# Expert results stored by token and choice, and the next mixers' input products by token tile and by half

## The chip, the cores and the metric

The kernel runs on one core of a Trainium2 chip. The metric is device microseconds of one execution. TensorE (PE) multiplies matrices, VectorE (DVE) and ScalarE (ACT) do elementwise work, GpSimd (POOL) does small operations and issues the DMAs that take a list of row indices, SyncE (SP) issues nearly all other loads and stores.

## The reference, cut to what matters

512 tokens of 1024 channels go through two blocks in fp32. The first block has two layers, a mixer (fox attention, then MLA attention) followed by 16 experts, of which each token uses the two best of its best group. The second block puts 16 meta tokens in front and has a Hyena convolution mixer and a differential attention.

```python
h = rmsnorm(x, mix_norm[i]) * (1.0 + sc1) + sh1
y = fox_mixer(h, ...) if i % 2 == 0 else mla_mixer(h, ...)
x = x + g1 * y
h = rmsnorm(x, ffn_norm[i]) * (1.0 + sc2) + sh2
x = x + g2 * hier_moe(h, ...)        # y = sum over a token's two choices of weight * expert(h)
...
y = rmsnorm_2(h, norm_pre[i])        # second block: h is 16 meta tokens, then x
u = y @ w_in + b_in                  # hyena: four streams of 2048 channels
x0, x1, v = jnp.split(dwconv_centred(u[..., :3 * D_INNER], conv_w, conv_b), 3, axis=-1)
```

So behind each expert layer stand the same steps: y of both choices is summed, multiplied by g2, added to x, and x is normed for the next mixer's input product.

## The kernel before, in words

**Order of the phases.** Fox attention of layer 0 (to about 350 us), experts of layer 0 (355 to 641), MLA (641 to 880), experts of layer 1 (920 to 1222), Hyena (1207 to 1890), differential attention (to the end). The instructions of a phase are written in Python; a scheduler then orders them on each engine by readiness and priority, and each engine works through its own list strictly in order. SyncE's queue, and POOL's, are such lists too. Tiles have tags with a fixed number of buffers, so a load may start only when the reader of the buffer's earlier content is done.

**Products in fp32** are three matmuls on split numbers (`mm3`, lines 147 to 153): each operand is a high part (ACT cast, line 125) and a low part (DVE subtraction, line 128). Weights come as `raw` (load by SyncE, line 133), then `whi` and `wlo`. `rsqrt` (lines 114 to 119) is one DVE operation and POOL's power.

**Experts** (`moe`, line 1096). The routing gives each token and choice a slot in one of 16 blocks of 128 (one per expert); blocks 16 to 22 take an expert's 129th slot and beyond. `tix` (line 1185) holds the token of each slot, for an empty slot the index of a spare row. For each block `gather` (line 1204) fetches 128 rows of `hd` by an indirect DMA (line 1206), `expert_in` and `expert_out` (lines 1061, 1076) make the products, ACT copies the result to `yo` (line 1092), and POOL issues an indirect DMA that adds the rows of `yo` into `yd` (line 1093). Since rows are added, `yd`, of 512 + 128 rows, must be zero first: `moe_fill` (lines 939 to 947), called twice in fox attention (lines 625, 627), stores 2560 KB of zeros into `yd` and 512 KB into the spare rows of `hd`, for each layer. Behind the 16 experts an If (line 1247) takes the first overflow block, and a For_i (line 1250) over `n_ov` takes further ones. Between the experts, and after that loop, parts of Hyena's filter network run as filler (`fil`, lines 1393 to 1409).

**The seam to MLA** (`mla`, from line 704). `moe_sum` (line 1261) loads `yd` by tile of 128 tokens. `moe_norm` (line 338) is a generator over the four tiles: y times g2 (lines 346 and 359), x plus y (345), square (ACT, into h; tile 0 by DVE, line 354), rsqrt, x times r times gain (360), plus shift (362), then `put_T` (line 368) transposes and splits. The input product of 672 columns goes by column half: `gemm_tok` (line 777) takes all four token tiles for columns 0 to 335, then all four for the rest; `evac_in` (line 766) copies to `ct` (line 774).

**The seam to Hyena** (`hyena`, from line 1430). The same, with no shift. Then the constants (`cw`, `hb`, `cb`, line 1467) and four tables (line 1297, by POOL's queue) are loaded. `streams(ct)` (line 1506) makes the four streams of a channel tile: `proj` (line 1483) takes both token halves of 264 columns for one stream, with 24 matmuls each, `conv` (line 1493) is a three-tap convolution on the result, copied out by ACT (line 1499). `long_conv` (line 1522; its first matmul is at line 1545) follows.

## Time and profile before

| | us |
|---|---|
| median of 3 runs | 2627.5 (2625.51 to 2631.35) |
| the profiled execution | 2622.27 |
| its span in the trace | 2620.5 |
| PE busy | 2384.9 (91%) |
| DVE busy | 1887.5 (72%) |
| ACT busy | 1507.4 (58%) |
| POOL busy | 255.4 (10%) |

The page of the profile gives busy time by engine, the span in 40 slices, the DMA queues, the chain of work that ended last and the costliest groups of instructions. The trace behind it answers for any stretch: windows (busy time of each engine, granted clock of PE, share of the DMA engines), waits (which line waited for what, how long in all), the timeline (one line for each instruction or run of like ones) and groups of instructions by shape. "A <- B" in a wait means that A stood until B was done. An engine with q behind its name is its queue of DMA and control instructions.

### The profile page before, as it was taken

Reading aid. Unit: us, or ns where it says so; the run is one execution under the profiler, and the core shown is the slowest. Engines: PE = TensorE matmul, PEld = TensorE weight load, DVE = VectorE, ACT = ScalarE, POOL = GpSimd, SP = SyncE. Lnnn points to the kernel's source line nnn. Section 1 sums busy time; section 2 is a strip of 40 time slices with the busy share of each in tenths; the row PEclk is TensorE's granted clock in tenths of the full one; section 3 lists DMA queues with packets and bytes.
Section 4 is the critical chain, followed back from the end, with each engine's and each line's share of the span. In section 5 each row is a group of like instructions: output and inputs, shape, how many; then the busy total and the mean of one; then the engine's idle time right before and its main releaser. Section 6 shows DMA issues by size and latency. Waiting matters only on the chain.

```text
span 2620.5 us, 40079 instructions
## 1 busy us (share of the span) xinstructions
PE 2384.9 (91%) x14775; PEld 1978.0 (75%) x14775; DVE 1887.5 (72%) x4037; ACT 1507.4 (58%) x2958; POOL 255.4 (10%) x264
## 2 busy tenths in 40 slices
PE   6889988897899979995999999999799999999988
PEld 5667767775766767774999999997577777777666
DVE  7888877886788768885566666664657778777755
ACT  5575757885567368874444444443336666665652
POOL 1100112221122022211000000000100000000000
PEclk8899989999899989997999999999899999999989
DMA  7776668997211289985323222224322121111232
GB/s 262 249 254 203 219 187 267 322 316 228 88 37 49 75 256 315 327 282 196 103 90 92 92 93 92 91 73 131 116 89 69 41 73 69 65 49 69 88 108 82
DMA packets 130271, 387.00 MB, mean 148 GB/s; under 512 B 23226, under 2 KB 34730, under 8 KB 129304
## 3 DMA queue, kind: packets, MB, share of 16 engines
q1 hardware_dynamic: 115640, 330.31, 37.1%
q0 software_dynamic: 12128, 45.38, 7.2%
q10 hardware_dynamic: 2304, 8.72, 0.8%
q8 instruction: 117, 1.92, 0.3%
q14 instruction: 82, 0.67, 0.1%
HBM read 330.58 MB, written 53.77 MB: 147 GB/s over the span
## 4 chain that ended last, share of the span: by engine, by line
PE 45%; DVE 4%; ACT 2%; issue 2%; DMA 1%; POOL 0%; POOLq 0%; SPq 0%; ACTq 0%; DVEq 0%
PE ps_mm L150 11%; PE ps_mm L151 10%; PE ps_mm L152 10%; PE ps_sc L1822 1%; PE ps_b L152 1%; PE ps_b L150 1%; PE ps_b L151 1%; PE ps_sc L1823 1%; PE ps_tp L1852 1%; ACT whi L125 1%; PE ps_tl L1764 1%; PE ps_tp L1565 1%; DVE wlo L128 1%; PE ps_pv L150 1%; PE ps_tq L1852 1%
## 5 line engine op out<-in xcount | busy, mean ns | idle before, releaser
L128 DVE TENSOR_TENSOR wlo<-raw,whi 128x1024 fp32r<-128x1024 f32 (+3 forms) x426 | 501.3, 1185 | 244.0 <-ACT whi L125 230.6
L125 ACT CAST whi<-raw 128x1024 fp32r<-128x1024 f32 (+3 forms) x426 | 433.2, 1022 | 246.9 <-PE ps_mm L152 91.1
L150 PE MATMUL ps_mm<-hT,whi 128*128 128x264 f32 x1024 | 294.7, 288 | 0.8 <-ACT hT L125 0.8
L151 PE MATMUL ps_mm<-hT,whi 128*128 128x264 f32 x1024 | 293.4, 287 | 0.8 <-DVE hT L128 0.8
L152 PE MATMUL ps_mm<-hT,wlo 128*128 128x264 f32 x1024 | 292.0, 285 | 0.0
L150 PE MATMUL ps_mm<-whi,hT 128*128 128x512 f32 x512 | 206.9, 406 | 6.9 <-DVE zg L1757 5.9
L151 PE MATMUL ps_mm<-wlo,hT 128*128 128x512 f32 x512 | 205.9, 403 | 0.0
L152 PE MATMUL ps_mm<-whi,hT 128*128 128x512 f32 x512 | 205.6, 403 | 0.0
L151 PEld LDWEIGHTS ps_mm<-hT,whi 128*128 128x128 f32 x1024 | 194.7, 190 | 1.1 <-DVE hT L128 1.1
L150 PEld LDWEIGHTS ps_mm<-hT,whi 128*128 128x128 f32 x1024 | 194.1, 190 | 1.6 <-ACT hT L125 1.6
L152 PEld LDWEIGHTS ps_mm<-hT,wlo 128*128 128x128 f32 x1024 | 194.4, 190 | 0.0
L151 PE MATMUL ps_mm<-wlo,un 128*128 128x384 f32 (+1 forms) x376 | 140.4, 375 | 10.0 <-DVE wlo L128 9.8
L150 PE MATMUL ps_mm<-whi,un 128*128 128x384 f32 (+1 forms) x376 | 141.4, 379 | 4.4 <-ACT whi L125 1.7
L152 PE MATMUL ps_mm<-whi,un 128*128 128x384 f32 (+1 forms) x376 | 138.3, 372 | 0.0
L1830 ACT ACTIVATE P<-P,nm 128x528 f32<-128x528 f32 x128 | 94.4, 737 | 70.7 <-DVE P L1827 69.1
L1499 ACT ACTIVATE u<-ps_mm,hb 128x264 f32<-128x264 f32 x96 | 46.2, 481 | 137.4 <-PE ps_mm L152 137.4
L119 POOL TENSOR_TENSOR r<-rs,mhalf 128x4 f32<-128x4 f32 (+1 forms) x72 | 79.1, 1102 | 400.1 <-DVE rs L118 381.5
L150 PEld LDWEIGHTS ps_mm<-whi,hT 128*128 128x128 f32 x512 | 97.0, 190 | 27.2 <-DVE zg L1757 6.8
L150 PE MATMUL ps_mm<-whi,xgT 128*128 128x512 f32 x264 | 107.1, 406 | 8.2 <-ACT xgT L125 8.2
L219 DVE CUSTOM_DVE_ANT_0 ada<-ada,crow 128x1024 f32<-128x1024 f32 x80 | 97.5, 1219 | 22.1 <-DMA ada<-in_w_ada_dram 21.4
L152 PEld LDWEIGHTS ps_mm<-whi,hT 128*128 128x128 f32 x512 | 97.0, 190 | 18.1
L151 PEld LDWEIGHTS ps_mm<-wlo,hT 128*128 128x128 f32 x512 | 96.8, 189 | 17.5 <-issue 0.2
(594 smaller groups left out, 6379.4 us busy)
## 6 DMA issues: line engine op xcount, KB each, us to landing
raw<-in_moe_gu_dram SPq DMA_DIRECT2D x136, 512.0 KB, 7.7
ada<-in_w_ada_dram SPq DMA_DIRECT2D x96, 512.0 KB, 4.3
raw<-in_moe_dn_dram SPq DMA_DIRECT2D x68, 512.0 KB, 7.0
raw<-in_hy_w_dram SPq DMA_DIRECT2D x64, 512.0 KB, 3.5
raw<-in_da_w_dram SPq DMA_DIRECT2D x64, 512.0 KB, 4.6
raw<-in_fox_w_dram SPq DMA_DIRECT2D x32, 384.0 KB, 4.6
hs<-ht ACTq DMA_DIRECT2D x16, 532.0 KB, 7.3
H<-hs SPq DMA_DIRECT2D x16, 532.0 KB, 3.4
```

Of the source, the lines that this page charges most:

```text
L119: self.lastpow = nc.gpsimd.tensor_tensor(out, t, self.mhalf[:in_.shape[0]].to_broadcast(list(in_.shape)), op=ALU.pow)
L125: nc.scalar.copy(hi, src)
L128: return nc.vector.tensor_sub(lo, src, hi.bitcast(F32))
L150: r = nc.tensor.matmul(o, a[0], b[0], start=first, stop=False)
L151: nc.tensor.matmul(o, a[0], b[1], start=False, stop=False)
L152: self.lastmm = nc.tensor.matmul(o, a[1], b[0], start=False, stop=last)
L219: nc.vector.tensor_tensor_reduce(out=t, in0=t, in1=self.crow, op0=ALU.mult, op1=ALU.add, scale=1.0, scalar=0.0, accum_out=v[:, j:j + 1])
L1499: A.activation(u[:, 1 + hs.start:1 + hs.stop], p, AF.Identity, bias=hb[:, c:c + 1])
L1565: nc.tensor.transpose(p[:, cs], ab[:, f, cs], self.ident)
L1764: nc.tensor.matmul(tp[32 * j:32 * j + 16, 0:64], xt[:, k, :], w[:, c0 + j * 64:c0 + (j + 1) * 64], start=(k == 0), stop=(k == KD - 1))
L1830: nc.scalar.activation(P, P, AF.Exp, bias=nm_, scale=-1.0, accum_out=sum_)
L1852: nc.tensor.transpose(p[0:n, qt * 128:(qt + 1) * 128], Ps[qt][:, kt * 128:kt * 128 + n], self.ident)
```

## The change

1. `yd` has 2 x 512 rows: a block's result row is stored, not added, at row choice x 512 + token. Empty slots get an index past the end, which the bounds check of the DMA skips. A third column of the table (`tix`) keeps the token for the gathers, which are bounds-checked too; as their empty rows are not written, the first three `xg` buffers of each layer are set to zero. `moe_fill` goes.
2. The loop over further overflow blocks stands in an If of its own.
3. `moe_sum` loads two halves of `yd`; `moe_norm` adds them, multiplies by g2, adds to x, squares on ACT into a scratch tile, multiplies by the gain, and, between rsqrt and the last operation, does the next tile's sum.
4. MLA's input product goes by token tile, both column halves for a tile as soon as it is normed; the weights of the second half are split ahead, in eight tiles of 336 columns.
5. Hyena's first channel tile goes by token half: after the norm of tiles 0 and 1 the first halves of all four streams, then the norm of tiles 2 and 3, then the second halves. The constants and tables are now written behind tile 0's norm. `conv`, `proj` and `streams` become generators; for later channel tiles the order is the same.

```diff
--- before.py
+++ after.py
...
             nc.tensor.transpose(p[:, k, :], h[:, k * 128:(k + 1) * 128], self.ident[:NM, :NM])
         nc.vector.tensor_mul(d, p, gcol[:, :, None].to_broadcast([128, KD, NM]))
-    def moe_norm(self, ys, gain, hT, c0, tags, shift=None):
+    def moe_norm(self, ys, junk, gain, hT, c0, tags, shift=None):
         nc, ph = self.nc, self.ph
         V = nc.vector
-        def add(t):
-            return V.tensor_add(self.x[t], self.x[t], ys[t])
-        V.tensor_mul(ys[0], ys[0], self.g2)
-        add(0)
+        def both(t):
+            y, pieces = ys[t]
+            n = D // len(pieces)
+            for i, p in enumerate(pieces):
+                V.tensor_add(y[:, i * n:(i + 1) * n], y[:, i * n:(i + 1) * n], p)
+            V.tensor_mul(y, y, self.g2)
+        both(0)
         for t in range(NT):
-            x, h = self.x[t], ys[t]
+            x, h = self.x[t], ys[t][0]
             ss, r = [self.sm.tile([128, 1], F32, tag=n, name=n) for n in ("ss", "rstd")]
-            if t:
-                nc.scalar.activation(h, x, AF.Square, accum_out=ss)
-            else:
-                V.tensor_tensor_reduce(out=h, in0=x, in1=x, op0=ALU.mult, op1=ALU.add, scale=1.0, scalar=0.0, accum_out=ss)
+            V.tensor_add(x, x, h)
+            nc.scalar.activation(junk(), x, AF.Square, accum_out=ss)
+            V.tensor_mul(h, x, gain)
             self.rsqrt(r, ss, 1.0 / D, EPS)
             if t < 2:
                 self.midpow = self.lastpow
             if t < NT - 1:
-                V.tensor_mul(ys[t + 1], ys[t + 1], self.g2)
-            m = V.scalar_tensor_tensor(h, x, r, gain, op0=ALU.mult, op1=ALU.mult)
-            if shift is not None:
-                m = V.tensor_add(h, h, shift)
-            if t < NT - 1:
-                self.order(add(t + 1), m)
+                both(t + 1)
+            if shift is None:
+                V.tensor_scalar(h, h, r, None, op0=ALU.mult)
+            else:
+                V.scalar_tensor_tensor(h, h, r, shift, op0=ALU.mult, op1=ALU.add)
             self.put_T(h, hT, c0 + t * 128, tags)
             yield t
...
                 more(1)
                 if g < 7:
                     proj(g + 1)
-                if g == 1:
-                    self.moe_fill(0)
-                if g == 6:
-                    self.moe_fill(1)
                 if g == MLPG:
                     for _ in self.hy_filter_mlp("PT", "sc"):
                         pass
...
             def four():
                 return [[ph.t([128, 4, S], F32R, "h4") for _ in range(2)] for _ in range(2)]
             w_in = lambda c: lambda b: I["mla_w"][c, 2 * b:2 * b + 2].rearrange("k p n -> p k n")
-            ys = [ph.t([128, D], F32, "qT", "y") for _ in range(NT)]
+            ys = [(ph.t([128, D], F32, "qT", "y"), [ph.t([128, D], F32, "PT", "y2")]) for _ in range(NT)]
             sh, A = [ph.t([128, D], F32, "v", n) for n in ("sh", "A")]
             self.moe_sum(0, 0, ys[0])
             self.mod_to(A, 1, 1)
...
             self.moe_sum(0, 3, ys[3])
             raws.append(self.raw(w_in(0)(2), 672))
             h4 = four()
-            for t in self.moe_norm(ys, A, h4, 0, ("tq", "tp"), sh):
+            hT = [[z[k // 4][:, k % 4, :] for k in range(KD)] for z in h4]
+            ws, ct = [[], []], {}
+            def split_in(c, b, raw):
+                if c:
+                    for j in range(2):
+                        w = [ph.t([128, 336], F32R, "qk", "w1") for _ in range(2)]
+                        self.split(*w, raw[:, j * 336:(j + 1) * 336])
+                        ws[c].append(w)
+                else:
+                    w = self.weights(raw, 672)
+                    ws[c] += [[z[:, j * 336:(j + 1) * 336] for z in w] for j in range(2)]
+            junk = lambda: ph.t([128, 1024], BF16, "sq", "junk")
+            for t in self.moe_norm(ys, junk, A, h4, 0, ("tq", "tp"), sh):
                 if t == 0:
-                    pre = [self.weights(z, 672, keep=True) for z in raws + [w_in(0)(3)]]
+                    for b in range(4):
+                        split_in(0, b, raws[b] if b < 3 else self.raw(w_in(0)(3), 672))
+                    for b in range(4):
+                        split_in(1, b, self.raw(w_in(1)(b), 672))
+                if t % 2 == 0:
+                    pair = ph.t([128, 2, 672], F32, "PT", "ct")
+                    ct[t], ct[t + 1] = pair[:, 0, :], pair[:, 1, :]
+                for c in range(2):
+                    p = ph.bank("mm")[:, :336]
+                    for k in range(KD):
+                        self.mm3(p, [z[k][:, t * 128:t * 128 + 128] for z in hT], ws[c][k], k == 0, k == KD - 1)
+                    nc.scalar.copy(ct[t][:, c * 336:(c + 1) * 336], p)
             self.dump("xm0", self.x)
-            hT = [[z[k // 4][:, k % 4, :] for k in range(KD)] for z in h4]
...
-            ct = {}
...
-            for c in range(2):
-                self.gemm_tok(hT, KD, w_in(c), 336, evac_in(c), pre=None if c else pre)
             lat = [[unit() for _ in range(5)] for _ in range(2)]
             kr, kss = {}, {}
             for t in range(NT):
...
         nc.gpsimd.iota(self.tok1, pattern=[[128, NT]], base=1, channel_multiplier=1,
                        allow_small_or_imprecise_dtypes=True)
...
         for c in range(2):
             nc.scalar.copy(yo[:, c * 512:(c + 1) * 512], acc[c])
         nc.gpsimd.indirect_dma_start(out=yd, out_offset=bass.IndirectOffsetOnAxis(ap=idx, axis=0),
-                                     in_=yo, in_offset=None, compute_op=ALU.add)
+                                     in_=yo, in_offset=None, bounds_check=2 * S - 1, oob_is_err=False)
...
                 R = ph.t([128, NT, 2, 23], F32, f"R{i}")
                 V.tensor_tensor(R[:, :, 0, :], self.iota[:, None, 0:23].to_broadcast(s23), b(tl, 23), op=ALU.is_equal)
                 V.tensor_mul(R[:, :, 1, :], R[:, :, 0, :], b(w, 23))
-                V.tensor_mul(R[:, :, 0, :], R[:, :, 0, :], b(self.tok1, 23))
+                V.tensor_mul(R[:, :, 0, :], R[:, :, 0, :], b((self.tok1, self.tok2)[i], 23))
...
+            tf = ph.t([128, 23, 3], F32, "tf")
             emp = ph.t([128, 23], F32, "emp")
-            V.tensor_scalar(emp, ptv[:, 0, :], 0.0, self.past, op0=ALU.is_equal, op1=ALU.mult)
+            V.tensor_scalar(emp, ptv[:, 0, :], 0.0, 4096.0, op0=ALU.is_equal, op1=ALU.mult)
             V.scalar_tensor_tensor(tf[:, :, 0], emp, -1.0, ptv[:, 0, :], op0=ALU.add, op1=ALU.add)
-            tix = ph.t([128, 23], I32, "tix")
-            V.tensor_copy(tix, tf[:, :, 0])
+            V.tensor_scalar(emp, tf[:, :, 0], S - 0.5, -float(S), op0=ALU.is_gt, op1=ALU.mult)
+            V.tensor_add(tf[:, :, 2], tf[:, :, 0], emp)
+            tix, tox = ph.t([128, 23], I32, "tix"), ph.t([128, 23], I32, "tox")
+            V.tensor_copy(tix, tf[:, :, 2])
+            V.tensor_copy(tox, tf[:, :, 0])
...
             def gather(idx):
                 xg = ph.t([128, D], F32, "xg")
+                if len(self.gathered) < 3:
+                    V.memset(xg, 0.0)
                 r = nc.gpsimd.indirect_dma_start(out=xg, out_offset=None, in_=hd,
-                                                 in_offset=bass.IndirectOffsetOnAxis(ap=idx, axis=0))
+                                                 in_offset=bass.IndirectOffsetOnAxis(ap=idx, axis=0),
+                                                 bounds_check=S - 1, oob_is_err=False)
...
             n_ov = nc.values_load(otab[0:1, 8:9], min_val=0, max_val=7)
             with tc.If(n_any > 0):
...
+            with tc.If(n_ov > 1):
+                with tc.For_i(1, n_ov, 1) as i:
+                    e = nc.values_load(otab[0:1, ds(i, 1)], min_val=0, max_val=15)
+                    ri = ph.t([128, 3], F32, "ri")
+                    nc.sync.dma_start(ri, tabd[:, ds(i + 16, 1), :].rearrange("p o n -> p (o n)"))
...
             for _ in fil:
                 pass
     def moe_sum(self, l, t, y):
-        self.nc.sync.dma_start(y, self.yd[l][t * 128:(t + 1) * 128, :])
+        whole, pieces = y
+        r = self.yd[l][t * 128:(t + 1) * 128, :]
+        self.nc.sync.dma_start(whole, r)
+        r, n = self.yd[l][S + t * 128:S + (t + 1) * 128, :], D // len(pieces)
+        for i, p in enumerate(pieces):
+            self.nc.sync.dma_start(p, r[:, i * n:(i + 1) * n])
...
                    "fsk isk fT0 fT1 fk ik uu0 uu1 fold sa y gate un", tmp="raw") as ph:
             h4 = [[ph.t([128, 4, T], F32R, "un", "hT") for _ in range(2)] for _ in range(2)]
             gain = ph.t([128, 4, FQ], F32, "H", "gain").rearrange("p a b -> p (a b)")[:, :D]
-            home = ("ab", "H", "abT", "T4")
-            ys = [ph.t([128, 4, FQ], F32, h, "y").rearrange("p a b -> p (a b)")[:, :D] if h == "H" else
-                  ph.t([128, D], F32, h, "y") for h in home]
+            t4 = ph.t([128, 4, 2, FQ], F32, "T4", "y").rearrange("p a b c -> p (a b c)")
+            two = lambda tag: [ph.t([128, T], F32, tag, "y2")[:, :512] for _ in range(2)]
+            ys = [(ph.t([128, D], F32, "ab", "y"), [ph.t([128, D], F32, "fsk", "y2")]),
+                  (ph.t([128, 4, FQ], F32, "H", "y").rearrange("p a b -> p (a b)")[:, :D], two("s")),
+                  (ph.t([128, D], F32, "abT", "y"), two("g")), (t4[:, :D], [t4[:, D:2 * D]])]
             for t in range(NT):
                 self.moe_sum(1, t, ys[t])
                 if t == 0:
                     self.bc_to(gain, I["norm_pre_2"][0])
             raws = {z: self.raw(I["hy_w"][0, z]) for z in (1, 2, 0)}
-            for t in self.moe_norm(ys, gain, h4, NM, ("tp",)):
-                if t == 0:
-                    for q in range(2):
-                        self.split(h4[0][q][:, :, 0:NM], h4[1][q][:, :, 0:NM], self.xmT[:, q * 4:q * 4 + 4, :])
-            self.dump("xm1", self.x)
+            junk = lambda: ph.t([128, D], BF16, "fold", "junk")
+            norm = self.moe_norm(ys, junk, gain, h4, NM, ("tp",))
+            next(norm)
+            for q in range(2):
+                self.split(h4[0][q][:, :, 0:NM], h4[1][q][:, :, 0:NM], self.xmT[:, q * 4:q * 4 + 4, :])
...
+            def streams(ct, halves=False):
+                ph_t = lambda tag, nm: ph.t([128, T], F32, tag, nm)
+                run = []
+                def go(g):
+                    run.append(g)
+                    if not halves:
+                        for _ in g:
+                            pass
+                    else:
+                        next(g)
+                x1, v = ph_t("s", "x1"), ph_t("s", "v")
+                go(conv(1, ct, x1))
+                go(conv(2, ct, v))
+                if not halves:
+                    V.tensor_mul(uus[ct % 2][:, 0:T], x1, v)
+                x0 = ph_t("y" if halves else "s", "x0")
+                go(conv(0, ct, x0))
+                zb, th = ph_t("g", "zb"), ph_t("g", "th")
...
+                if halves:
+                    yield
+                    for i, g in enumerate(run):
+                        for _ in g:
+                            pass
+                        if i == 1:
+                            V.tensor_mul(uus[ct % 2][:, 0:T], x1, v)
...
-            streams(0)
+            next(norm)
+            begun = streams(0, True)
+            next(begun)
+            for _ in norm:
+                pass
+            self.dump("xm1", self.x)
+            for _ in begun:
+                pass
             for ct in range(CH):
                 long_conv(ct)
                 if ct < CH - 1:
-                    streams(ct + 1)
+                    for _ in streams(ct + 1):
+                        pass
```

## Rows read from the trace of the kernel before

**Rows 1.** Windows: length, PE, PEld, DVE, ACT, POOL busy, PEclk, DMA share, GB/s.
```profile
405.00:633.00 228.00, 208.71 (x1064) 169.70 (x1063) 185.41 (x286) 180.23 (x300) 52.34 (x41) 0.99 0.92 296
...
644.00:681.00 37.00, 24.04 (x116) 20.13 (x115) 32.15 (x56) 14.20 (x26) 3.13 (x4) 0.79 0.52 166
...
1200.00:1220.00 20.00, 7.82 (x27) 5.52 (x27) 9.21 (x16) 5.08 (x11) 2.29 (x3) 0.57 0.67 211
```

**Rows 2.** SyncE queue waits, 900 to 1207: total us, times, longest.
```profile
SPq L133 <- DVE wlo L128: 120.5, 64, 7.2
SPq L1250 <- DMA yd<-yo,tix: 36.3, 3, 20.1
```

**Rows 3.** Engine waits, 1160 to 1215: total us, times, longest.
```profile
ACT feo L1372 <- DMA yd<-yo,tix: 7.4, 1, 7.4
...
ACT yo L1092 <- DMA yd<-yo,tix: 2.9, 1, 2.9
```

**Rows 4.** Timeline, 633 to 700: start, us, engine line operation, [idle before <- releaser].
```profile
633.37 1.56 POOL L1093 DMA_INDIRECT yd<-yo,tix  x1 [5.59 <-ACT yo L1092]
...
640.78 0.35 SPq L1263 DMA_DIRECT2D y<-yd  x1
...
644.74 1.23 DVE L346 TENSOR_TENSOR y<-y,gate 128x1024 f32<-128x1024 f32 x1 [3.43 <-DMA y<-yd]
...
653.69 0.32 SPq L1263 DMA_DIRECT2D y<-yd  x1
...
680.31 0.68 DVE L128 TENSOR_TENSOR h<-ps_tp,h 128x512 fp32r<-128x512 f32 x1
...
684.13 0.44 ACT L774 COPY ct<-ps_mm 128x336 f32<-128x336 f32 x1
...
699.41 0.43 ACT L774 COPY ct<-ps_mm 128x336 f32<-128x336 f32 x1
```

**Rows 5.** Timeline of seam 2, the same columns.
```profile
1200.52 1.55 POOL L1093 DMA_INDIRECT yd<-yo,tix  x1 [18.56 <-ACTq L1250]
...
1207.47 0.34 SPq L1263 DMA_DIRECT2D y<-yd  x1
...
1214.33 1.23 DVE L346 TENSOR_TENSOR y<-y,gate 128x1024 f32<-128x1024 f32 x1
...
1219.36 1.48 POOL L119 TENSOR_TENSOR rstd<-rs,mhalf 128x1 f32<-128x1 f32 x1 [10.22 <-DVE rs L118]
...
1227.18 0.54 POOL L119 TENSOR_TENSOR rstd<-rs,mhalf 128x1 f32<-128x1 f32 x1 [6.34 <-DVE rs L118]
...
1228.64 0.21 DVE L1467 TENSOR_TENSOR cb<-cw,hb 128x48 f32<-128x48 f32 x1 [1.54 <-DMA cw<-in_hy_conv_dram]
...
1234.10 0.59 PE L150 MATMUL ps_mm<-hT,whi 128*128 128x264 f32 x1 [0.76 <-ACT hT L125]
...
1240.33 0.48 ACT L1499 ACTIVATE u<-ps_mm,hb 128x264 f32<-128x264 f32 x1 [5.80 <-PE ps_mm L152]
...
1265.04 0.28 PE L150 MATMUL ps_mm<-hT,whi 128*128 128x264 f32 x1
...
1266.01 0.28 PE L152 MATMUL ps_mm<-hT,wlo 128*128 128x264 f32 x1
...
1272.25 0.36 PE L1545 MATMUL ps_b<-fsk,fk 73*128 73x266 f32 x1 [0.18 <-issue]
```

**Rows 6.** DMA issues by kind: count, KB each, median us to landing.
```profile
y<-yd SPq DMA_DIRECT2D x8, 512.0 KB, 6.1
...
yd<-yo,tix POOLq DMA_INDIRECT x33, 9.7
```

**Rows 7.** Groups of DVE by shape: count, busy us, mean ns.
```profile
L345 DVE TENSOR_TENSOR x<-x,y 128x1024 f32<-128x1024 f32 x8 | 9.8, 1220 | 0.1
...
L473 DVE MEMSET wf<- 128x1024 f32 x2 | 1.8, 912 | 0.3 <-issue 0.3
```

**Rows 8.** SyncE queue waits, 100 to 170: total us, times, longest.
```profile
SPq L946 <- DVE mlp L689: 3.9, 1, 3.9
```

62 lines of the change are left out of this document (18 added, 44 removed).

## The prediction, made before the changed kernel was built

> **What bounds the kernel now.** I read the windows by stage first, then the waits at the two places where an expert layer hands over to the next mixer (the seams), then the timeline there. PE is busy 91% of the profiled span of 2620.5 us, so a gain must come from stretches in which PE is not fed. In the first expert layer PE works 208.7 of 228 us at a clock of 0.99, DVE 185.4, ACT 180.2, while the DMA share is 0.92 [rows 1]: PE leads there, and only 19 us are free in all. The seams are the weak places. From 644 to 681 PE is busy 24.0 of 37 us at a clock of 0.79 and DVE 32.2: DVE's norm chain leads. From 1200 to 1220 PE has 7.8 of 20 us at 0.57, and DVE 9.2 [rows 1]: there every engine waits. SyncE's queue stood at the loop over further overflow experts (line 1250) for 36.3 us in three waits on the scattered expert results [rows 2], and ACT, whose next work had nothing to do with them, waited 7.4 us for the same landing [rows 3].
>
> Seam 1 in time [rows 4]: the last scatter is issued at 633.37, the first y load at 640.78, the first multiply of y runs at 644.74, the last piece of tile 3's normed input is ready at 680.31 + 0.68 = 680.99; column half 0 of the last tile is copied out at 684.13 + 0.44, half 1, whose 96 matmuls all stand behind half 0, at 699.41 + 0.43 = 699.84. Seam 2 [rows 5]: scatter 1200.52, y load 1207.47, first operation on y 1214.33, first projection matmul 1234.10, first half's copy 1240.33; the first transform matmul, at 1272.25, comes when the four streams of channel tile 0 are through.
>
> **The sum, part by part,** is made against the profiled execution, 2622.3 us; the median of the runs is 2627.5, 5.2 more, and the gain is carried over to the median unchanged.
>
> *A, seam 1, gain 6 (1 to 9).* Neither layer has a second overflow expert (33 scatters are 16 + 16 + 1 [rows 6]), so the loop is skipped, and its entry with it. Then the y loads go out when the last scatter has landed. From that scatter's issue to the first y load 7.4 us passed (633.37 to 640.78), landing and entry together. About half the slots are empty (1024 results for 16 x 128), so half the bytes go: the saving lies between nothing (no part of the 7.4 goes by bytes or by the entry) and 3.7 (all of it by bytes). I take 3, nearer the upper end since the entry goes too, and give 0.3 back for the second half's 0.5 MB (1.8 us at the 296 GB/s of the expert stage [rows 1], most of it beside the first half): the first operation on y at 642 in place of 644.74. DVE then has more to do: one 128x1024 pass more per tile (add y2, times gate, add to x, times gain, final, against four before), 4 x 1.22 [rows 7] = 4.9; tile 0's square leaves it for ACT, -1.2; the eight splits of half 1 (336 columns) move ahead of the last norm, 8 x 0.5 (an estimate between 0.21 for 48 columns [rows 5] and 1.22 for 1024 [rows 7]) = 4.0. Together +7.7, against -2.7 from the start; DVE's idle time in that window was 37 - 32.15 = 4.85 [rows 1], of which I let 2 be filled. Tile 3's last piece: 681 + 7.7 - 2.7 - 2 = 684. What is then left is one tile, both halves, 48 matmuls: half 1's 96 took 699.84 - 684.57 = 15.3, so 48 take 7.6, and with the transposes ahead and the copy behind it ends about 693: 699.8 - 693 = 6.8, less 0.8 for waits on POOL's power. Lower end: a scatter no faster and only 0.7 of the idle time filled (1); upper end: all 3.7 of the scatter and 4.2 of the idle time (9).
>
> *B, seam 2, gain 10 (4 to 14).* The y loads leave when the overflow expert's scatter has landed, but now the filter work behind the loop (1207.6 to about 1221) runs meanwhile: the 7.4 us of ACT's wait [rows 3] are filled. Tile 0 is normed no earlier than the y load lets it; the constants, which tile 1's chain of before met at 1228.64 with a wait of 1.54 [rows 5], stay where they are. The first operation on y, 1214.33 before, I put 4 earlier, since that tail is out of its way; tiles 0 and 1 carry two passes more and a final one of about 0.75 (an estimate by columns, as above) for one of 1.2, some 2 each, less tile 0's square, +2.8: the first matmul at 1234.1 - 4 + 2.8 = 1233 (1231 to 1234). From there PE has 96 matmuls for the first half of the tokens while tiles 2 and 3 are normed, then 96 for the second, in place of two bursts of 24 with a wait between. Eight steps took 1266.01 - 1265.04 = 0.97, 0.121 each [rows 5]: 192 x 0.121 = 23.3; the first 24 at half clock, 6.2 (1234.10 to 1240.33) in place of 2.9, +3.3; transposes of two tiles between, +2.5. 1233 + 29 = 1262 against 1272.25. If the second half waits for tile 3 (two tiles x 8.4 us from about 1240) it begins at 1257 and ends at 1268: gain 4.
>
> *C, layer 1's last scatters, gain 2 (0 to 3).* ACT's yo copy waited once 2.9 us for an earlier scatter to leave its buffer [rows 3]. An empty slot is skipped; with about half the slots empty that landing is earlier.
>
> *D, the fills, gain 1 (0 to 4).* Two stores of 2560 KB and two of zeros into hd leave fox attention. SyncE waited 3.9 once for their source [rows 8], with other loads behind it; whether PE came to wait for those no row shows: between 0 and 3.9, I take 1, since most loads run ahead of their use. The 6.3 MB themselves, 21 us at 296 GB/s, went beside PE's work.
>
> *E, new work in the expert layers, cost 2 (0 to 6.6).* Three small DVE operations in each routing, about 0.2 each (cb, 128x48, took 0.21 [rows 5]), 6 x 0.2 = 1.2 on the path; six memsets of 128x1024, 6 x 0.912 [rows 7] = 5.5, on a DVE that is 81% busy while gathers wait anyway: between 0 and 5.5, I take 0.8 of it.
>
> *F, the bounds check on 63 indirect DMAs.* No row shows it. A scatter takes POOL 1.56 [rows 4]; an expert's period is 228/16 = 14.3 us, and POOL works 52.3 of 228 [rows 1]; with one gather and one scatter per expert they are hidden up to some 7 us for each. It may also be less, since fewer descriptors go out; I take 0, its bound stands with the slower rival. Plain writes instead of accumulated ones, and the skipped rows, halve this queue's traffic; in a stage that PE leads this gains nothing (0 to the second rival's 10).
>
> Sum: 6 + 10 + 2 + 1 - 2 = 17. **2627.5 - 17 = 2610.5.** All the best ends: 9 + 14 + 3 + 4 = 30, 2597.5; all the worst: 1 + 4 - 6.6 = -1.6, 2629.
>
> Two rules are set against rows. POOL's power of tile 0 took 1.48 us beside DVE's tensor operations, tile 1's 0.54 [rows 5]; beside the next tile's adds it may be held by them, by up to 0.94 for each of 8 tiles, 7.5. The Trainium skill, SBUF — State Buffer, section Who interferes with whom, says that DVE and GpSimd share one pair of ports under an exclusive lock. By that, the trace agrees in direction: 1.48 against 0.54. By that rule every power beside such an operation is held, an estimate of half of 7.5 on the path, and the sum would be about 4 us smaller; by the rows, in which one of these two was not held, I charged 0.8. For the scatters, the row shows 9.7 us from issue to landing in the median [rows 6], and the last of layer 0 at most 7.4 [rows 4]. The Trainium skill, DMA: Bandwidth & Descriptors, section Anatomy of one DMA — SWDGE (gpsimd) path, gives a fixed 2.0 us plus bytes over 436e3, an estimate of 2.6 us for a half-empty scatter; the trace disagrees for the full ones (3.2 by the rule). By the rule A would gain about 1 more, by the rows what the sum has.
>
> **Rivals.** *DVE's order takes the seams' gain (2621.5).* DVE led in 644-681 [rows 1], and the change gives it more to do; then A and B come out at their low ends: 1 + 4 + 2 + 1 - 2 = 6. Against it: half of B doesn't hang on DVE. Chance 0.16. *The experts gain too (2600.5).* The DMA share is 0.92 [rows 1]; if part of the 19 us in which PE isn't busy there is due to late weights, half of it in each layer, some 5 x 2, goes with the indirect traffic. Against it: DVE and ACT free the buffers SyncE waits for (120.5 us in 64 waits in layer 1 [rows 2]), not the queue. 0.10. *The change doesn't take the barrier away (2614.5):* the If around the loop syncs as the loop did; A and B lose 4 together. 0.06. *Slower (2636): the splits of half 1 block DVE.* They are written ahead of tile 1's norm, and DVE works in its issued order. Their eight loads (8 x 0.69 MB) stand behind 4.2 MB of y, 9.7 MB in all; at 296 GB/s [rows 1] from 640 that is 33 us, the last lands about 673. Three tiles at 8.4 us each ((32.15 - 3.4)/4 + 1.2, the 3.4 an estimate for half 0's splits) would follow: 674 + 25 = 699, and 7.6 us of matmuls, near 707 to 708: +8. The constants (cb) ahead of tile 1 of seam 2 do the same, their load behind doubled y loads: +1.5 in place of -10, the rest -1: +8.5. It decides if the last raw lands after about 665 and the splits are really issued before tile 1. For it: the fourth y load left only at 653.69 [rows 4]. Against it: the order on an engine needn't be the program's, and the splits of half 0 sat between the norms without leaving DVE idle. A check that costs POOL over 7 us each would end on this side too. 0.10.
>
> **How the numbers follow.** Forecast 0.58, rivals 0.16, 0.10, 0.06, 0.10. A measurement of this kernel can tell about 0.2%, 5.3 us, from no change. Faster by more: 0.58 + 0.10 + 0.06 + 0.04 (a quarter of the first rival, which lies on the edge) = 0.78; within: 0.12; slower: 0.10. The range takes in the best ends and the second rival below, the first rival and most bad ends above: 2597 to 2625; outside it are the slower rival and some tails.
>
> **What would show it.** Right: no event of the further-experts loop on any queue; y loads at most 6 us after the last scatter while filter matmuls run; the last ct copy near 692; the first transform matmul near 1262; POOL's indirect DMAs still near 1.6 us; the expert period near 14.3. Wrong: DVE waits for raw of half 1 ahead of tile 1's add; ct copies later than 700; the first half of stream 0 followed by a long PE wait for tile 3; or a scatter above 7 us on POOL.

## The result, and the profile after

The changed kernel takes 2641.8 us in the median of nine runs, the kernel before 2624.2 in nine runs on the same chips; the ratio is 1.0073 (1.0058 to 1.0088): slower by 19 us, where 17 us faster was forecast. One of the changed kernel's nine runs took 5839 us and is left out of the ratio. The two traces can be laid beside each other by events that both have:

| event | before | after | difference |
|---|---|---|---|
| layer 0: indices of the first gather ready | 404.86 | 400.17 | -4.7 |
| first gather issued | 405.14 | 404.85 | -0.3 |
| second scatter issued | 442.33 | 447.43 | +5.1 |
| last scatter issued | 633.37 | 637.28 | +3.9 |
| MLA: last input product copied out | 699.84 | 702.20 | +2.4 |
| layer 1: first gather issued | 961.02 | 964.00 | +3.0 |
| second scatter issued | 995.83 | 1004.99 | +9.2 |
| last scatter issued | 1200.52 | 1204.08 | +3.6 |
| Hyena: first stream product | 1234.10 | 1256.99 | +22.9 |
| first transform product | 1272.2 | 1291.2 | +19.0 |
| last instruction | 2620.5 | 2644.0 | +23.5 |

The right column says where to look: it jumps at the first experts of both layers (by 9.8 from 400 to 447, and by 6.2 from 964 to 1005) and at seam 2 (by 19.3 from the last scatter to the first product), and falls a little in between. The profiled run of after is 3.9 us above its own median, so the last line is somewhat large.

The first gather of layer 0 in the changed kernel (timelines of DVE, POOL and PE: start, duration, engine, line, operation, [idle before <- releaser]), and last the filter's first product in layer 1:

```profile
400.01 0.16 DVE L1187 CAST tix<-tf 128x23 int32<-128x23 f32 x1
...
403.65 0.91 DVE L1211 MEMSET xg<- 128x1024 f32 x1 [0.15 <-issue]
...
404.85 3.63 POOL L1212 DMA_INDIRECT xg<-hd,tix  x1 [27.33 <-DVE th L1072]
408.48 0.62 POOL L1349 DMA_DIRECT2D fst<-fstd  x1
...
416.28 1.25 PE L1384 MATMUL ps_fl<-fst,fw 128*128 128x264 f32 x4 [5.79 <-DMA fst<-fstd]
...
975.49 1.25 PE L1384 MATMUL ps_fl<-fst,fw 128*128 128x264 f32 x4 [6.39 <-DMA fst<-fstd]
```

The filter's first product of layer 0 in the kernel before, and the windows from 425 to 450 of the kernel before and of the changed kernel (length, then PE, PEld, DVE, ACT, POOL busy, PEclk, DMA share, GB/s):

```profile
417.82 0.75 PE L1370 MATMUL ps_fl<-fst,fw 128*128 128x264 f32 x4 [2.06 <-DMA fst<-fstd]
...
425.00:450.00 25.00, 22.60 (x116) 18.51 (x115) 22.92 (x34) 21.72 (x34) 5.80 (x5) 1.00 1.00 294
...
425.00:450.00 25.00, 21.17 (x95) 17.04 (x94) 19.91 (x32) 18.63 (x30) 4.54 (x5) 0.86 0.79 246
```

The indices (`tix`) are there at 400.17. The gather leaves at 404.85, when the memset of its buffer, which DVE did behind two weight splits, has ended at 404.56. (The view names `th`, which ended at 404.84, as the releaser. Where no memset stands in between, the gather follows its indices by 0.28 us, in the kernel before and in no_memset below; 0.28 behind the memset's end is 404.84 too.) The load of the filter's table (`fst`) stands behind that gather on POOL's queue, and PE, which was 5.3 us ahead of the kernel before at 410 (its transposes of `th` start at 410.05, before at 415.32), waits 5.8 us for it. In the kernel before the same wait was 2.06. It is followed by a lower clock: the 128x512 products behind that wait take 0.63 us each to 421 and 0.39 from 422 on, and from 425 to 450 the granted clock is 0.86, before it was 1.00.

Seam 1 of the changed kernel by windows (columns as above):

```profile
644.00:681.00 37.00, 22.21 (x106) 19.06 (x105) 29.72 (x36) 13.32 (x26) 3.49 (x3) 0.72 0.77 256
670.00:680.00 10.00, 9.93 (x62) 9.40 (x61) 8.66 (x13) 4.74 (x11) 1.46 (x1) 0.97 0.51 150
680.00:690.00 10.00, 9.72 (x64) 9.00 (x63) 9.15 (x31) 6.16 (x20) 3.00 (x5) 1.00 0.36 115
690.00:702.00 12.00, 11.35 (x77) 11.05 (x76) 8.13 (x37) 7.42 (x18) 1.12 (x2) 1.00 0.22 62
```


The same stretch in the timeline, from the last scatter to the last copy of the input product:

```profile
637.28 0.97 POOL L1092 DMA_INDIRECT yd<-yo,tox  x1 [5.60 <-ACT yo L1091]
...
642.42 0.34 SPq L1274 DMA_DIRECT2D y<-yd  x1
...
647.52 1.23 DVE L348 TENSOR_TENSOR y<-y,y 128x1024 f32<-128x1024 f32 x1 [7.21 <-DMA y<-yd]
...
657.77 0.65 PE L150 MATMUL ps_mm<-whi,h 128*128 128x336 f32 x1 [0.92 <-ACT h L125]
...
701.77 0.43 ACT L752 COPY ct<-ps_mm 128x336 f32<-128x336 f32 x1
```

Against [rows 4] the y load comes 5.1 us behind the last scatter instead of 7.4, about as forecast, but the first sum 10.2 behind it where the first multiply was 11.4. The first of the 192 products runs at 657.77, and by 670 PE has done 17 of them. From 670 on it has no gap worth naming (9.93 of 10, 9.72 of 10, 11.35 of 12): PE, not the last tile's norm, sets the end. From the last scatter to the end of the last copy it is 64.9 us in place of 66.5.

Seam 2 of the changed kernel: the waits of SyncE's queue from 1200 to 1295 (total us, times, longest).

```profile
SPq L1277 <- PE ps_fl L1421: 7.2, 1, 7.2
...
SPq L1277 <- DVE fk L1298: 4.7, 1, 4.7
```

Its window from 1210 to 1220 (columns as above):

```profile
1210.00:1220.00 10.00, 7.77 (x27) 5.62 (x25) 0.68 (x1) 4.35 (x9) 0.00 (x0) 0.66 0.00 0
```

And its timeline, from the first load of y to the first stream product:

```profile
1206.75 0.33 SPq L1274 DMA_DIRECT2D y<-yd  x1
...
1219.07 0.33 SPq L1277 DMA_DIRECT2D y<-yd  x1
...
1223.65 1.23 DVE L348 TENSOR_TENSOR y<-y,y 128x1024 f32<-128x1024 f32 x1 [11.86 <-DMA y<-yd]
...
1235.98 1.04 ACT L125 CAST whi<-raw 128x1024 fp32r<-128x1024 f32 x1 [0.58 <-DMA raw<-in_hy_w_dram]
...
1236.77 4.35 POOL L119 TENSOR_TENSOR rstd<-rs,mhalf 128x1 f32<-128x1 f32 x1 [1.94 <-DVE rs L118]
...
1248.97 0.21 DVE L1483 TENSOR_TENSOR cb<-cw,hb 128x48 f32<-128x48 f32 x1 [6.92 <-DMA cw<-in_hy_conv_dram]
...
1252.12 1.04 ACT L125 CAST whi<-raw 128x1024 fp32r<-128x1024 f32 x1 [7.46 <-DMA raw<-in_hy_w_dram]
...
1254.34 0.75 DVE L363 TENSOR_SCALAR y<-y,rstd 128x1024 f32<-128x1024 f32 x1
...
1255.23 1.94 PE L375 MATMUL ps_tp<-ident,y 128*128 128x128 f32 x8 [22.07 <-DVE y L363]
...
1256.99 0.81 PE L150 MATMUL ps_mm<-hT,whi 128*128 128x264 f32 x2
```

The first half of tile 0 is loaded at 1206.75, 2.7 us after the scatter and earlier than in [rows 5]. Its second half leaves at 1219.07: its buffer (`fsk`) lies where the filter tail still works, and SyncE stands 4.7 us for DVE and 7.2 us for PE. All further loads of y stand behind it, and from 1210 to 1220 the DMA engines move nothing. Then DVE waits 6.92 us for `cw`, and PE 22.07 us for tile 1. Tile 1's power is done at 1241.12 (1236.77 + 4.35), but the last operation of its norm runs only at 1254.34: in DVE's list it stands behind the constants (`cb`) and the splits of four weights, and the fourth of these weights lands at 1252.12. The first weight was there at 1235.98.

### The profile page after: what moved, and what is told of

Read it like the earlier page. It is cut to its first block, busy times and chain, and to the rows that moved or that the text cites. A ratio compares the mean times of both kernels' runs of the same rounds, so it can differ in the third digit from the quotient of the medians.

```text
span 2644.0 us, 40098 instructions
## 1 busy us (share of the span) xinstructions
PE 2392.1 (90%) x14775; PEld 1983.7 (75%) x14775; DVE 1902.9 (72%) x4061; ACT 1511.3 (57%) x2966; POOL 243.7 (9%) x264
## 5 line engine op out<-in xcount | busy, mean ns | idle before, releaser
L128 DVE TENSOR_TENSOR wlo<-raw,whi 128x1024 fp32r<-128x1024 f32 (+2 forms) x422 | 498.2, 1189 | 231.9 <-ACT whi L125 222.4
L125 ACT CAST whi<-raw 128x1024 fp32r<-128x1024 f32 (+2 forms) x422 | 430.1, 1025 | 278.1 <-PE ps_mm L152 115.8
L150 PE MATMUL ps_mm<-whi,xgT 128*128 128x512 f32 x264 | 110.2, 418 | 8.5 <-ACT xgT L125 8.5
L152 PE MATMUL ps_mm<-whi,xgT 128*128 128x512 f32 x264 | 109.6, 415 | 3.0 <-DVE xgT L128 3.0
L151 PEld LDWEIGHTS ps_mm<-wlo,hT 128*128 128x128 f32 x512 | 96.9, 189 | 17.5 <-issue 0.2
```

The costliest lines, as they stand in the source:

```text
L125: nc.scalar.copy(hi, src)
L128: return nc.vector.tensor_sub(lo, src, hi.bitcast(F32))
L150: r = nc.tensor.matmul(o, a[0], b[0], start=first, stop=False)
L151: nc.tensor.matmul(o, a[0], b[1], start=False, stop=False)
L152: self.lastmm = nc.tensor.matmul(o, a[1], b[0], start=False, stop=last)
```

## The experiments

Each kernel is timed against the kernel before on the same chip; the changed kernel is at 1.0073 on this scale, and 0.001 is 2.6 us. The kernel before has medians of 2621.0 (the first four lines of the table), 2624.6 (the next four) and 2621.6 (the last four), so differences between runs are taken from the ratios.

| kernel | median, us | ratio to before (95%) |
|---|---|---|
| y2_swap | 2635.9 | 1.0058 (1.0041 to 1.0075) |
| no_memset | 2625.5 | 1.0021 (1.0010 to 1.0031) |
| consts_first | 2640.5 | 1.0075 (1.0058 to 1.0092) |
| all_three | 2623.8 | 1.0007 (0.9996 to 1.0019) |
| tables_late | 2610.7 | 0.9954 (0.9938 to 0.9970) |
| final_first | 2625.8 | 1.0002 (0.9992 to 1.0012) |
| fill_back | 2650.5 | 1.0101 (1.0081 to 1.0121) |
| for_plain | 2644.4 | 1.0073 (1.0054 to 1.0092) |
| tables_only | 2629.9 | 1.0032 (1.0011 to 1.0054) |
| whole_streams | 2617.7 | 0.9991 (0.9979 to 1.0004) |
| col_halves | 2613.4 | 0.9974 (0.9962 to 0.9986) |
| both_fixed | 2606.2 | 0.9953 (0.9937 to 0.9970) |

**y2_swap.**

```diff
-ys = [(ab, [fsk]),     (H, two("s")), ...
+ys = [(ab, two("s")),  (H, [fsk]),    ...
```

> Edit: the second halves of y of tiles 0 and 1 change places at the Hyena seam, so that tile 0's no longer lies in the buffer that the filter tail reads. Theory: the change loses at this seam because SyncE stands 11.9 us (4.7 on DVE's fk, 7.2 on PE's last filter matmul) before the second half of tile 0 can be loaded. Then the first sum of halves starts near 1212 in place of 1223.65 in the profile, and the time falls by 6 to 12 us, to 2630 to 2636. Rival (the doubled loads themselves and the waiting constants set this seam): the first sum moves, but cb still ends on cw near 1249 and the time stays within 3 us of 2641.8.

1.0058: 4 us, less than the 6 to 12 expected, and its interval meets that of the changed kernel. The stand of SyncE is still there (6.6 and 2.8 us), now ahead of tile 1's half. The first product comes at 1256.04. The first sum comes 7.7 us behind the last scatter (1206.26 to 1213.99) in place of 19.6, and the first product still 49.8 behind it in place of 52.9: what the late half held back is then held by something else, and its own 4 us are not shown beyond the noise.

**no_memset.**

```diff
-if len(self.gathered) < 3:
-    V.memset(xg, 0.0)
-V.tensor_copy(tix, tf[:, :, 2])
+V.tensor_scalar(tix, tf[:, :, 2], float(S - 1), None, op0=ALU.min)
```

> Edit: empty slots gather token 511 (index clamped by the cast that made it anyway), and the three memsets of xg in each layer go. Theory: the first memset, in DVE's order behind two weight splits, holds the first gather 4.4 us after its indices are ready (400.17 to 404.85), the filter's table load stands behind the gathers on POOL's queue, and PE waits 5.8 us for it (6.4 in layer 1) and then runs some us at a lower clock. Then that PE wait falls to about 1 us or less in both layers, and the time falls by 12 to 20 us, to 2622 to 2630. Rival (the order of PE's list, shuffled by the change, put the filter too early whatever the gathers do): the wait stays at 4 us or more and the time falls by less than 5 us.

1.0021: 14 us, as the first theory had it. The timelines at the first gather and at the filter's first product:

```profile
402.44 0.16 DVE L1187 TENSOR_SCALAR tix<-tf 128x23 int32<-128x23 f32 x1
...
402.88 3.48 POOL L1209 DMA_INDIRECT xg<-hd,tix  x1 [23.47 <-DVE ot L1196]
406.36 0.62 POOL L1346 DMA_DIRECT2D fst<-fstd  x1
...
415.97 1.25 PE L1381 MATMUL ps_fl<-fst,fw 128*128 128x264 f32 x4 [3.07 <-DMA fst<-fstd]
...
964.04 0.75 PE L1381 MATMUL ps_fl<-fst,fw 128*128 128x264 f32 x4 [1.03 <-DMA fst<-fstd]
```

The gather now follows its indices by 0.3 us (402.60 to 402.88), as before the change. PE's wait falls from 5.79 to 3.07 in layer 0, more than the 1 us expected, and from 6.39 to 1.03 in layer 1. The other traces say the same: in the six kernels with the memsets this wait is 4.2 to 6.2 us in layer 0 and 5.8 to 6.8 in layer 1, in the seven without them 0.4 to 3.1 and 0.5 to 2.3.

**consts_first.**

```diff
+hb, cw loaded here
 for t in range(NT):
     self.moe_sum(1, t, ys[t])
...
-hb, cw loaded here
```

> Edit: Hyena's two constant loads (hb, cw) are issued ahead of the loads of y instead of behind them and the weights. Theory: DVE's wait of 6.9 us at cb (for cw, to 1248.97) goes, and with it most of the wait of tile 1's norm, but the 11.9 us ahead of tile 0's second half stay: 4 to 7 us faster, 2635 to 2638. Rival (the wait at cb only hides the wait for weights, which land late in the same queue): under 2 us.

1.0075, nothing: the rival. DVE's wait at cb is gone from the list of waits, and the first product comes at 1256.26, in the changed kernel at 1256.99. Tile 1's last operation still stands behind the splits of four weights, and the fourth lands at 1251.38 (in the changed kernel at 1252.12): the wait at `cw` only hid the wait for the weights.

**all_three.**

> The three edits together: second halves swapped, no memsets, constants first. Theory: what they save adds up, since they sit in three places, 22 to 32 us: 2610 to 2620, faster than the kernel before (2624) by some 4 to 14. Rival: the seam's gains overlap (whatever ends one wait uncovers the next, the weights), 2622 to 2632.

1.0007: less than the first theory, the rival's 2622 to 2632. The last scatter now comes at 1186.67, 13.9 us ahead of the kernel before, and the first transform product at 1272.5, as in the kernel before: seam 2 takes 85.8 us, before 71.7. The windows of all_three (columns as above):

```profile
1200.00:1210.00 10.00, 3.00 (x14) 2.18 (x12) 2.77 (x4) 3.58 (x8) 3.49 (x6) 0.76 0.60 216
1210.00:1220.00 10.00, 0.00 (x0) 0.00 (x0) 5.76 (x10) 1.15 (x2) 2.13 (x13) 0.50 1.06 414
1220.00:1230.00 10.00, 0.00 (x0) 0.00 (x0) 3.94 (x4) 2.31 (x3) 0.00 (x0) 0.50 0.96 329
```


The timeline of the same stretch has the first of the tables' loads, and what was waited for:

```profile
1204.22 0.94 POOL L1308 DMA_DIRECT2D fwd_hi<-in_k_fwd_hi_dram  x1
...
1217.54 0.56 POOL L119 TENSOR_TENSOR rstd<-rs,mhalf 128x1 f32<-128x1 f32 x1 [5.97 <-DVE rs L118]
...
1225.83 1.23 DVE L348 TENSOR_TENSOR y<-y 128x1024 f32<-128x1024 f32 x1 [6.32 <-DMA y<-yd]
...
1227.26 1.05 ACT L125 CAST whi<-raw 128x1024 fp32r<-128x1024 f32 x1 [12.84 <-DMA raw<-in_hy_w_dram]
...
1235.62 0.74 DVE L363 TENSOR_SCALAR y<-y,rstd 128x1024 f32<-128x1024 f32 x1
```

PE has nothing to do from 1210 to 1230, and the DMA engines are full at 414 and 329 GB/s. Among what they move are the four tables, issued by POOL from 1204.22 to 1206.78 behind tile 0's power; in the kernel before they stood behind tile 1's, from 1228.28. A half of y and the first weights land at 1225 to 1227. Tile 1's power is done at 1218.10, and its last operation runs at 1235.62, again behind the sums of tiles 2 and 3 and the splits of four weights in DVE's list. That gave the next two experiments.

**tables_late.**

```diff
 next(norm)                      # tile 0
 ...
+next(norm)                      # tile 1
 fwd = self.table("fwd", ...)
 ...
-next(norm)
 begun = streams(0, True)
```

> all_three with one more step: the four tables, and all that follows them, are written behind tile 1's norm (as in the kernel before) instead of behind tile 0's. In all_three the DMA engines are full from 1208 to 1229 (share 1.06 and 0.96) while PE has nothing to do (0 us of 20), and the tables' 4.3 MB lie in that stretch beside the halves of y and the weights. Theory: at this seam the transfers set the time, and the tables, needed only some 60 us later, take 4.3 MB / 0.4 MB per us = 10 us of it: 5 to 10 us faster than all_three, 2614 to 2619. Rival (DVE's order sets it: tile 1's last operation stands behind the sums of tiles 2 and 3 and behind weight splits): within 3 us of 2623.8.

0.9954: 14 us better than all_three, more than the 5 to 10 expected, and faster than the kernel before by 12 us. The tables leave at 1214.45, and the first product comes 32.0 us after the last scatter, in all_three 51.6 (timeline of tables_late):

```profile
1213.38 1.05 ACT L125 CAST whi<-raw 128x1024 fp32r<-128x1024 f32 x1 [0.45 <-DMA raw<-in_hy_w_dram]
...
1214.45 0.95 POOL L1308 DMA_DIRECT2D fwd_hi<-in_k_fwd_hi_dram  x1
...
1214.53 0.75 DVE L363 TENSOR_SCALAR y<-y,rstd 128x1024 f32<-128x1024 f32 x1 [0.44 <-POOL rstd L119]
...
1217.19 0.81 PE L150 MATMUL ps_mm<-hT,whi 128*128 128x264 f32 x2
...
1256.67 0.36 PE L1580 MATMUL ps_b<-fsk,fk 73*128 73x266 f32 x1
```


Its windows behind that:

```profile
1210.00:1220.00 10.00, 3.23 (x13) 2.73 (x14) 9.56 (x15) 5.36 (x7) 5.39 (x17) 0.50 0.92 344
1220.00:1230.00 10.00, 10.00 (x67) 10.00 (x67) 4.42 (x4) 1.15 (x3) 0.00 (x0) 0.78 1.05 414
```

The transfers are as dense as they were (0.92 and 1.05), but those that PE waits for come first: the first weight is cast 28.2 us behind the last scatter, in all_three 40.6, and PE is busy 10 of 10 us from 1220. The edit did a second thing: tile 1's norm, written ahead of the tables, is now also ahead of the constants and the splits in DVE's list, and its last operation follows its power by 0.03 us (1214.50 to 1214.53), in all_three by 17.5. Both rivals of the expectation are therefore at work, and no run has one without the other. An estimate from the traces: the late weights alone would have held the first product of all_three to about 42 us behind the last scatter (the first weight's high part is ready at 1228.31), and DVE's order makes up the rest to 51.6.

**final_first.**

```diff
-if t < NT - 1:
-    both(t + 1)
 V.tensor_scalar(h, h, r, None, op0=ALU.mult)
+if t < NT - 1:
+    both(t + 1)
```

> all_three with the last operation of a tile's norm issued ahead of the next tile's sum of halves instead of behind it. In all_three tile 1's power is there at 1218.1, its last operation runs at 1235.62, since DVE stands 6.3 us for a half of y and then splits weights; PE waits 29.5 us for it. Theory by DVE's order: tile 1 is ready near 1220, PE then waits for the weights (raw lands at 1227, split by 1229.6) and the first product starts near 1230 in place of 1238.5: 5 to 8 us faster at this seam, less about 0.6 us at each of the other tiles, 2617 to 2621. Rival (transfers set it): within 3 us of 2623.8, or slower, since POOL's power is then no longer hidden behind the next sum.

1.0002, the rival's time, but the edit did not test DVE's order. The scheduler put the same operations in the same order around tile 1 as in all_three: its power is done at 1219.36, and its last operation runs at 1236.76, still behind the sums of tiles 2 and 3 and the splits of four weights.

**tables_only.**

> The changed kernel with only the tables' step moved back behind tile 1's norm; memsets, the place of the second halves and the constants are as in the changed kernel. If the tables' start is a cause by itself, this gives 8 to 13 us (the step from all_three to tables_late gave 13.0): 2629 to 2634. If it only pays once tile 0's second half is no longer late (the tables then follow late halves anyway), under 4 us: 2638 to 2642.

1.0032: 11 us by this step alone, so the place of the step is a cause by itself, also with the late half still there. With no_memset's 14 and y2_swap's 4 that makes 29 of the 31 us from the changed kernel to tables_late. Its timeline says by which way:

```profile
1236.45 0.95 POOL L1311 DMA_DIRECT2D fwd_hi<-in_k_fwd_hi_dram  x1
1236.53 0.75 DVE L363 TENSOR_SCALAR y<-y,rstd 128x1024 f32<-128x1024 f32 x1 [0.44 <-POOL rstd L119]
...
1239.19 0.81 PE L150 MATMUL ps_mm<-hT,whi 128*128 128x264 f32 x2
```

The first weight is cast 32.1 us behind the last scatter (1203.34 to 1235.48), in the changed kernel 31.9: here the tables do not delay it. What moves is tile 1's last operation, from 1254.34 to 1236.53, out from behind the constants and the weight splits in DVE's list. The weights whose splits it stood behind do land later among the tables (the second and third are cast 35.7 and 39.5 us behind the last scatter, here by 33.2 and 36.5), so order and transfers work together in the changed kernel; how the 11 us divide between them is open.

**whole_streams.**

```diff
-begun = streams(0, True)
-next(begun)
 for _ in norm:
     pass
-for _ in begun:
+for _ in streams(0):
     pass
```

> tables_late with the first channel tile's four streams made whole, behind all four norms, as in the kernel before; the doubled loads and the new norm stay. Theory of the prediction (PE fills the norm of tiles 2 and 3 with the first halves): 6 to 12 us slower, 2617 to 2623; in tables_late PE has 96 products of this kind between 1218 and 1235. Rival (the halves' transfers and the weights set the seam, whichever way the products go): within 3 us of 2610.7.

0.9991, 10 us slower than tables_late, as the theory had it. From the first product to the first transform product it takes 47.9 us, in tables_late 39.5 (1217.19 to 1256.67). The timeline of whole_streams:

```profile
1219.30 0.59 PE L150 MATMUL ps_mm<-hT,whi 128*128 128x264 f32 x1
...
1267.16 0.36 PE L1580 MATMUL ps_b<-fsk,fk 73*128 73x266 f32 x1 [0.16 <-issue]
```

So the half order saves 8 to 10 us against whole streams in the same kernel. But the stretch itself is not the 29 us of the sum, and no shorter than in the kernel before (38.2).

**col_halves.**

```diff
-for c in range(2):              # per tile
-    products and copy of tile t, half c
+for c in range(2):              # behind all norms
+    for t in range(NT):
+        products and copy of tile t, half c
```

> tables_late with MLA's products by column half again (all tiles for columns 0 to 335, then all for the rest); the early splits stay. The trace of the changed kernel has PE busy from 670 to 702 nearly without a gap, so the order by tile can save little at the last copy; it lets the latents of the early tiles begin sooner. Theory: 2 to 5 us slower, 2613 to 2616. Rival: within 1.5 us.

0.9974, 5 us slower than tables_late, within the theory's 2 to 5; the intervals touch, but the trace says the same: from the last scatter to the last copy 70.2 us (628.74 to 698.97), in tables_late 65.7 (626.06 to 691.77).

**fill_back.**

> The changed kernel with the two zero fills put back where the kernel before had them (2560 and 512 KB each, into rows of yd that are written again later). The traces put the fills' removal at 4.8 us by the end of fox attention. Theory: that gain is real but is eaten at the first gather, which the memset holds at the same time in both: the time stays within 3 us of 2641.8, while the last additions to x in front of the first expert layer come 4 to 5 us later than in the changed kernel. Rival: the fills cost their full 4 to 5 us, 2646.

1.0101, some 7 us slower than the changed kernel; the intervals touch. It points to the rival, that the fills' cost is not hidden at the first gather, but how much they cost is open: y2_swap, which has the changed kernel's fox attention unaltered, issues its first gather at 409.12 where the changed kernel's trace has 404.85, so that single traces differ by 4 us there. All traces together say a little more: the last addition to x in front of the first expert layer starts at 367.9 to 373.5 in the twelve kernels without the fills (371.0 in the mean), and at 374.0 and 375.6 in the two with them.

**for_plain.**

```diff
-with tc.If(n_ov > 1):
+if True:
     with tc.For_i(1, n_ov, 1) as i:
```

> The changed kernel without the If around the loop over further overflow blocks. The trace of the changed kernel shows a second, short wait at the If (PE 1.1 us, and the y load 5.1 us after the last scatter against 7.4 before). Theory: the loop's entry waits for the scatter, so without the If the y loads come later by 2 to 3 us at the first seam, and the filter tail of layer 1 starts some 3 us later: 3 to 6 us slower, 2645 to 2648. Rival (the If itself syncs all engines, and the loop adds nothing): within 2 us of 2641.8.

1.0073, the same. The loop's entry does make ACT wait: 3.7 us for the scatter, in the changed kernel 0.3. The loads of y at seam 2 wait for the same scatter either way (they leave at 1201.06, 3.3 us behind it, in the changed kernel 2.7), so 0.6 us is all that the entry could add there.

**both_fixed.**

```diff
-t3 = (t4[:, :D], [t4[:, D:2 * D]])
+t1 = (H, [t4[:, D:2 * D]]);  t3 = (t4[:, :D], [fT0, fT1])
 for t in range(NT):
     self.moe_sum(1, t, ys[t])
+    if t == 1:
+        raws = ...               # the first three weights, ahead of tiles 2 and 3
```

> tables_late with two steps more: tile 1's second half takes the unused half of tile 3's buffer (tile 3's goes into two buffers of the transform), so that no load of y waits for the filter tail's buffers (13.3 us without an issue on SyncE's queue, 1189.80 to 1203.10, in tables_late), and the first three weights are loaded ahead of tiles 2 and 3. Theory: the first product moves from 1218 to 1206 to 1212 and the time falls by 4 to 9 us, to 2602 to 2607. Rival (DVE's work on the tiles then sets it): under 3 us.

0.9953: no difference to tables_late by ratio (its median is 4.5 us lower, that of the kernel before 3.0), which is the rival's under 3 us. The first product comes 32.8 us behind the last scatter (1187.11 to 1219.87), in tables_late 32.0. The first weight is cast 4 us earlier than there (1209.31), but DVE works without a gap from 1208.14 on and reaches tile 1's last operation at 1217.21, as the rival has it. The gap on SyncE's queue is still there, 1191.75 to 1204.65, with the second half in another buffer (the queue's wait, 1185 to 1230):

```profile
SPq L1274 <- DMA hs<-ht: 12.5, 1, 12.5
```


The issues on either side of it, in the timeline:

```profile
1191.75 0.37 SPq L1271 DMA_DIRECT2D y<-yd  x1
1204.65 0.32 SPq L1274 DMA_DIRECT2D y<-yd  x1
```

So the shared buffer, which I had named, is not what holds this load once tile 0's half is out of the way; it waits for the landing of the filter's result (`hs`), as it did for 10.1 us in tables_late, and why it does was not tried.

## Why the prediction was wrong

The sum was -17; the changed kernel is at +19. By its parts:

*A, seam 1, gain 6 forecast:* 1.5 by the trace. The start came as reckoned, and the order by tile is worth about 4.5 us at the last copy (col_halves). That order only paid back what else the seam lost. The step that failed is "What is then left is one tile", 48 matmuls: the loads of half 0's weights lie between and behind the loads of y (the first issued at 645.33, the others from 655.29 on), so that the products of tile 0 were not done while the later tiles were normed, and PE worked through 175 of the 192 from 670 on.

*B, seam 2, gain 10 forecast:* lost 15.4 (+3.6 to +19.0). The term that failed is the start, "the first matmul at 1234.1 - 4 + 2.8 = 1233": it came at 1256.99, and the stretch from there to the first transform product took 34.2 us where the sum had 29. Two steps behind that term were wrong. The first operation on y, put 4 us earlier, came 9.3 later (1223.65), since the sum had no term for the buffer that tile 0's second half waits for; that costs some 4 us by y2_swap's ratio, within the noise. And the sum let the constants "stay where they are" and gave the tables' step no price, though the change writes both ahead of tile 1's norm. That alone costs 11 us (tables_only), 14 with the other delays gone: the tables' loads crowd those that PE needs, and tile 1's last operation falls behind constants and weight splits in DVE's list. How much each does is not separated. The filter tail does run at once, as forecast, and it is just this tail that holds the buffer. With both steps mended the seam is as long as before and no shorter, 71.5 us in tables_late against 71.7; with whole streams it takes 80.4 (1186.78 to 1267.16). So what is left of the change there costs some 8.7 us, and the half order pays just that back. That it is the doubled loads of y and the added sums is not shown.

*C* was right in kind: the copies of `yo` no longer wait for a landing. From its second scatter to its last, layer 1 takes 199.1 us in place of 204.7, a gain of 5.6 with 2 forecast; what of it comes from those copies was not tried. *D* was probably too low: 1 forecast, some 7 by fill_back with intervals that touch, some 4 by the traces at the end of fox attention.

*E, cost 2 (0 to 6.6) forecast:* 14 measured (no_memset). The memsets were counted and priced rightly (six of 0.91 us), but as load on a busy engine. The failing step is "while gathers wait anyway": the first gather waited for nothing but its indices, and behind it on POOL's queue stood the load that PE's next product needed. A memset of 0.9 us, behind two splits, moved that chain by 4.4 us; without it PE's wait is shorter by 2.7 us in layer 0 and 5.4 in layer 1. The clock behind the wait was lower too, 0.86 for 1.00 from 425 to 450 in layer 0.

*F* was right to take 0: POOL takes less for a scatter, 0.97 us for the last of layer 0 (1.56 in [rows 4]), and the median landing is 6.5 us in place of the 9.7 in [rows 6].

Of the rivals, the slower one (0.10, 2636) came nearest in time, and its mechanism held at one of its two places. At seam 2 DVE's list did stand behind constants whose load came late, for 6.9 us in place of the 1.5 it had, with tile 1's last operation behind them; but the constants alone were not it, since without their wait that operation stood behind the weight splits just as long (consts_first). At seam 1 the splits of MLA's half 1 did not block: DVE's longest wait on them was 1.0 us. The rival that the experts gain too was wrong for the kernel as changed, since they lost at their entry, more than they gained behind it. With the memsets gone it looks right in kind: from the first gather to the last scatter tables_late takes 224.4 us in layer 0 (before 228.2) and 233.3 in layer 1 (before 239.5), though among the seven traces without memsets these go up to 229.7 and 237.6. The rival that the barrier stays did not hold either: for_plain shows that the If spares ACT 3.4 us of waiting, though no time came of it.

The range, 2597 to 2625, would have held tables_late and both_fixed, but as far as seam 2 goes that is luck, since nothing is gained there. What makes tables_late faster than the kernel before lies ahead of that seam: its last scatter of layer 0 comes 7.3 us earlier, that of layer 1 15.3 (1185.18), and the first transform product 15.6.

## What to carry to other kernels

When a step is moved in a program whose engines and queues work in order, price what it lets start and what it puts behind it, not only what it does: transfers that start earlier without being needed earlier take the DMA engines from those that are, and an operation that falls behind one that waits for such a transfer waits with it. An operation that initialises a buffer belongs where the engine is idle, or should be made needless (here by clamping an index in a cast that ran anyway), since the first use of the buffer stands at the head of a chain. And a borrowed buffer is free only if its last reader is done when the load is issued: look at what stands on the queue behind that load.

## What the runs showed of the hardware that was not expected

A bounds-checked plain scatter with about half its rows skipped takes POOL less than an accumulating one that stores all rows (0.97 us against 1.56 for the last of layer 0; medians of all scatters 1.02 and 1.61), and lands earlier (6.5 against 9.7 us). Whether the skipped rows or the plain write do this is not separated.

One tiny power on POOL (128x1) took 4.35 us at 1236.77, where 0.54 to 1.48 had been seen [rows 5]. It ran beside four DVE operations on 512 or 1024 columns that followed each other without a gap, and ended 0.44 us after the last of them (1240.68); in consts_first one took 3.21 us and ended 0.43 after three such operations, in both_fixed one took 2.67 and ended 0.41 after three. The eight powers of the two seams took 11.5 us together, before 6.3; the prediction charged 0.8 for that.
